# Strassen steps of 512 columns in the down projection, with transfers that add

## The chip, the cores and the metric

The kernel runs on one core of a Trainium2 chip. Its time is the device time of one execution in microseconds. Three runs before the change gave 2172.07, 2172.8 and 2175.01 us, a median of 2172.8 us. The profile is of another single execution.

## The reference: what is computed

The program is a decoder trunk of two layers on 256 tokens of width 2048, all in float32. A layer computes `h = rmsnorm(x)`, projects h by `w_in`, runs latent attention (8 heads) and retention (8 heads) on the parts, joins them, and adds `mixed @ w_o` to x. Then comes the part that the change touches:

```python
h = rmsnorm(x, mlp_norm[l])
x = x + jnp.square(jax.nn.relu(h @ w_up[l])) @ w_down[l]   # 2048 -> 8192 -> 2048
```

After the second layer a last rmsnorm gives the output.

## The kernel before, in words

**Precision by parts.** Weights arrive in float32. Each is split into a rounded head (ScalarE, a cast, L194) and the rest (VectorE, `raw - head`, L195). A product is three partial products: head x head, head x rest, rest x head. In a plain projection (`mac_feat`, L226) head x head and head x rest are one matmul of 512 columns (L228), since the activation tile holds head and rest side by side, 256 tokens each; rest x head is one of 256 columns (L229).

**x and its tiles.** x lies transposed in SBUF: 16 tiles `x[j]` of 128 features by 256 tokens. The inner width of 8192 is handled in four blocks of `FB` = 2048 per layer (loop over b). In each block, 16 up tiles are made in groups of `UP_TILES` = 4: `proj_feat` makes them in PSUM, `relu_sum` joins the two halves and applies relu, `next_u` squares, scales and splits them into `us[k]`. For each two of them `next_f` makes the token-side sums that Strassen's scheme needs (`fs`). The last group is late: its tiles are finished while the down projection starts.

**The down projection of a block.** Part of its 2048 output columns goes by Strassen's seven products, the rest by plain tiles.
- A Strassen step takes two row tiles of `w_down` (256 rows) and 2 x `SB` columns. `second_factors` (L699) loads the two rows of blocks into two `raw` buffers, splits w11, w21 and w22, forms four sums in place on VectorE (L715) and splits those. `seven_products` (L721) runs 7 x 3 matmuls of `SB` columns (L729) into seven PSUM banks. A block has 8 steps.
- After each step stands one plain tile of 128 columns (`next_tile`, L806): two loads of 512 KB, two splits, 16 pairs of matmuls, then a join (L246, L247) and an add into `x[j]` (L811). With `SB` = 384 the steps cover 6 column tiles, and 10 tiles are plain: eight stand between the steps, two after them. In the last block seven stand between, two after `join_products`, one after `add_blocks`.
- After the last step of a block `gather_products` adds the seven banks to seven SBUF sums (copies in the first block). In a layer's last block `join_products` forms the result and `add_blocks` transposes it on TensorE and adds it to x; `done_x` then prepares x for the next stage.

**Buffers and order.** All weights pass through five `raw` buffers (`N_RAW`), filled by SP's queue in program order as buffers come free, and seven buffers of split weights (`N_SPLIT`). `tmp` has six tiles. Instructions are written in program order, and a scheduler that goes by its own cost estimates sets the order on each engine: among those ready by its estimate, the earlier in the program goes first. On the chip each engine then works strictly in that order. POOL does nothing after the first 39 us.

Of the kernel before, what the change touches and what calls it, by code (L numbers as in the profile page):

```python
# [15 lines left out]
ALU = mybir.AluOpType  # L16
# [16 lines left out]

UP_TILES = 4
OUT_GROUPS = [(0, 4), (4, 4), (8, 4), (12, 2), (14, 2)]


SB = 384
SN = 2 * SB // P
TILE_AFTER, LAST_TILE_AFTER = range(8), range(7)  # L40
N_RAW, N_SPLIT = 5, 7

# [51 lines left out]
def kernel(ctx: ExitStack, tc: tile.TileContext, xt, positions, w_in, w_uq, w_ukv, w_o, w_up, w_down,  # L94
# [20 lines left out]
    def w_tile(shape, moving=False):  # L115
        n = math.prod(shape[1:])
        o = MOVING if moving else 0
        t = wpool.tile([P, max(n, 2048) + 2 * MOVING], F32R, tag="w", name="w", bufs=N_SPLIT)[:, o:o + n]
        names = "abc"[:len(shape) - 1]
        return t.rearrange(f"p ({' '.join(names)}) -> p {' '.join(names)}", **dict(zip(names, shape[1:])))  # L120
# [229 lines left out]
    for l in range(DEPTH):  # L350
# [305 lines left out]
        with tc.tile_pool(name=f"mlp{l}", bufs=1) as up:  # L656
# [42 lines left out]
            def second_factors(r0):  # L699


                raws = [w_load(w_down[l][r0 + k * P:r0 + (k + 1) * P, 0:2 * SB], [P, 1, 2 * SB])[:, 0, :] for k in range(2)]
                w11, w12, w21, w22 = (r[:, n * SB:(n + 1) * SB] for r in raws for n in range(2))
                out = []
# [6 lines left out]

                parts([w11], w11)
                parts([w21, w22], raws[1])
                for dst, other in ((w11, w12), (w12, w22), (w22, w11), (w21, w22)):
                    nc.vector.tensor_tensor(dst, dst, other, op=ALU.add)  # L715
                parts([w11, w12], raws[0])
                parts([w21, w22], raws[1])
                weave()
                return out

            def seven_products(ps, us, f, k, factors, first, last):  # L721


                w11, w21, w22, t1, t3, t4, t2 = factors
                a11, a12, a22 = us[2 * k][:, :, 0:P], us[2 * k + 1][:, :, 0:P], us[2 * k + 1][:, :, P:T]
                s1, s3, s2, s4 = (f[:, :, i, :] for i in range(4))
                for i, a, w in ((1, a11, w11), (2, a12, w21), (3, s4, w22), (5, s1, t1), (7, s3, t3), (6, s2, t2), (4, a22, t4)):
                    for n, (p, q) in enumerate(((0, 0), (0, 1), (1, 0))):
                        nc.tensor.matmul(ps[i], a[:, p, :], w[:, q, :], start=first and n == 0, stop=last and n == 2)  # L729

            def gather_products(ps, sums, first):
                for i in (1, 2, 3, 5, 7, 6, 4):
                    if first:
# [27 lines left out]
            for b in range(FF // FB):  # L761
# [21 lines left out]

                for c in range(0, FB - UP_TILES * P, UP_TILES * P):
                    if end and c == UP_TILES * P:
                        add_blocks(join_products(sums, sums), False)
                    for i, ps in enumerate(proj_feat(w_up[l], 0, b * FB + c, ms, UP_TILES)):
                        next_u(relu_sum(ps))
                        if i % 2:
                            next_f()  # L790
                pss = proj_feat(w_up[l], 0, (b + 1) * FB - UP_TILES * P, ms, UP_TILES)
                factors = second_factors(b * FB)
# [13 lines left out]
                def next_tile():  # L806
                    j = tiles.popleft()
                    ps, = proj_feat(w_down[l], b * FB, j * P, us, 1)
                    t = tmp()
                    join(ps, t)  # L810
                    nc.vector.tensor_tensor(x[j], x[j], t, op=ALU.add)  # L811
                    if end:
                        done_x(j)

                pp = {i: bank()[:, 0:SB] for i in (1, 2, 3, 5, 7, 6, 4)}
                steps = FB // (2 * P)
# [68 lines left out]
```

## Time and profile before

| what | value |
|---|---|
| median of three runs | 2172.8 us |
| profiled execution, its own time | 2171.46 us |
| its span, first to last instruction | 2169.7 us |
| TensorE busy | 2140.7 us (99%) |
| VectorE busy | 1770.0 us (82%) |
| ScalarE busy | 1275.3 us (59%) |
| POOL busy | 24.2 us (1%) |
| transfer engines, SP's queue | 61.4% of 16 engines' span |

PE is TensorE, PEld its weight loads, DVE VectorE, ACT ScalarE. Matmuls are pipelined, so a matmul's own duration (0.39 us for 512 columns) is longer than the distance to the next one's start. The distance counts.

### The profile page before, as it was taken

The page shows a single profiled execution, that of the slowest core. Times are in us where ns is not written, and L with a number is a line of the kernel's source. Part 1 is how long each engine was busy: PE and PEld are TensorE (multiplying, and loading weights), DVE is VectorE, ACT ScalarE, POOL GpSimd, SP SyncE. Part 2 cuts the span into 40 slices and gives each one's busy share as a digit, 9 for nine tenths or more (in the row PEclk, how much of TensorE's full clock was granted, in tenths as well). Part 3 has the DMA queues.
Part 4 walks back from the last instruction along what each step waited for, and adds up shares of the span by engine and source line. Part 5 has one row for each costly group of instructions (what it writes and reads, how often), then busy time and mean ns, then how long its engine had stood idle before and what let it go on. Part 6 is the DMA issues. An engine that isn't in the chain of part 4 may idle for free.

```text
span 2169.7 us, 33889 instructions
## 1 busy us (share of the span) xinstructions
PE 2140.7 (99%) x12422; PEld 1915.4 (88%) x12422; DVE 1770.0 (82%) x3335; ACT 1275.3 (59%) x2234; POOL 24.2 (1%) x34
## 2 busy tenths in 40 slices
PE   7999999999999999999999999999999999999998
PEld 6888888889888889988988888888898898898897
DVE  8878976789679779879978888676896896798797
ACT  7555545566565566566655555456665665655665
POOL 4000000000000000000000000000000000000000
PEclk9999999999999999999999999999999999999999
DMA  8555556656756855864675565566486477567554
GB/s 248 179 161 177 146 189 195 184 147 204 233 151 182 241 165 170 250 179 136 206 209 154 169 176 159 185 190 184 136 250 195 143 211 230 147 192 228 168 170 139
DMA packets 367846, 400.16 MB, mean 184 GB/s; under 512 B 13120, under 2 KB 271296, under 8 KB 367680
## 3 DMA queue, kind: packets, MB, share of 16 engines
q1 hardware_dynamic: 366720, 397.08, 61.4%
q8 instruction: 97, 1.59, 0.3%
q10 hardware_dynamic: 960, 0.92, 0.1%
q14 instruction: 69, 0.57, 0.1%
HBM read 395.85 MB, written 2.10 MB: 183 GB/s over the span
## 4 chain that ended last, share of the span: by engine, by line
PE 86%; DVE 8%; ACT 3%; issue 1%; DMA 1%; SPq 0%; ACTq 0%; DVEq 0%
PE mm L228 45%; PE mm L229 24%; PE mm L729 6%; DVE w L195 3%; PE mm L233 3%; DVE raw L715 2%; PE mm L234 1%; PE at L228 1%; ACT w L194 1%; PE at L229 1%; DMA raw<-w_in 1%; ACT tb L246 1%; DVE t L767 1%; PE at L499 0%; PE at L498 0%
## 5 line engine op out<-in xcount | busy, mean ns | idle before, releaser
L194 ACT CAST w<-raw 128x1024 fp32r<-128x1024 f32 (+5 forms) x952 | 871.2, 932 | 694.2 <-PE mm L229 393.4
L195 DVE TENSOR_TENSOR w<-raw,w 128x1024 fp32r<-128x1024 f32 (+4 forms) x952 | 1014.5, 1079 | 305.7 <-ACT w L194 296.9
L228 PE MATMUL mm<-xs,w 128*128 128x512 f32 x2944 | 1033.5, 394 | 9.2 <-ACT w L194 7.5
L229 PE MATMUL mm<-xs,w 128*128 128x256 f32 x2944 | 825.9, 281 | 5.1 <-DVE w L195 4.9
L228 PEld LDWEIGHTS mm<-xs,w 128*128 128x128 f32 x2944 | 553.2, 188 | 129.1 <-ACT w L194 7.8
L229 PEld LDWEIGHTS mm<-xs,w 128*128 128x128 f32 x2944 | 554.8, 189 | 8.1 <-DVE w L195 7.6
L228 PE MATMUL mm<-u,w 128*128 128x512 f32 x1280 | 448.5, 392 | 0.7 <-DVE t L247 0.7
L229 PE MATMUL mm<-u,w 128*128 128x256 f32 x1280 | 360.6, 282 | 4.0 <-DVE w L195 4.0
L228 PEld LDWEIGHTS mm<-u,w 128*128 128x128 f32 x1280 | 240.2, 188 | 50.1 <-DVE t L247 1.0
L229 PEld LDWEIGHTS mm<-u,w 128*128 128x128 f32 x1280 | 241.2, 188 | 8.4 <-DVE w L195 8.0
L228 PE MATMUL mm<-mix,w 128*128 128x512 f32 x512 | 178.0, 392 | 0.0
L246 ACT COPY tb<-mm 128x256 f32<-128x256 f32 x296 | 106.2, 370 | 77.1 <-PE mm L229 72.9
L715 DVE TENSOR_TENSOR raw<-raw 128x384 f32<-128x384 f32 x256 | 142.5, 557 | 6.7
L729 PE MATMUL mm<-w,f 128*128 128x384 f32 x768 | 143.9, 336 | 0.0
L229 PE MATMUL mm<-mix,w 128*128 128x256 f32 x512 | 143.8, 281 | 0.0
L729 PEld LDWEIGHTS mm<-w,f 128*128 128x128 f32 x768 | 134.4, 188 | 0.1
L247 DVE TENSOR_TENSOR t<-mm,tb 128x256 f32<-128x256 f32 x296 | 118.9, 418 | 16.8 <-ACT tb L246 15.3
L729 PE MATMUL mm<-w,u 128*128 128x384 f32 x576 | 121.9, 337 | 0.0
L228 PEld LDWEIGHTS mm<-mix,w 128*128 128x128 f32 x512 | 96.1, 188 | 20.9
L729 PEld LDWEIGHTS mm<-w,u 128*128 128x128 f32 x576 | 98.9, 188 | 2.9 <-ACT w L194 0.3
L229 PEld LDWEIGHTS mm<-mix,w 128*128 128x128 f32 x512 | 96.5, 188 | 0.0
L233 PE MATMUL mm<-w,xs 128*128 128x512 f32 x256 | 92.7, 401 | 0.0
(196 smaller groups left out, 1694.4 us busy)
## 6 DMA issues: line engine op xcount, KB each, us to landing
raw<-w_up SPq DMA_DIRECT2D x256, 512.0 KB, 4.4
raw<-w_down SPq DMA_DIRECT2D x160, 512.0 KB, 5.0
raw<-w_in SPq DMA_DIRECT2D x144, 512.0 KB, 4.5
raw<-w_down SPq DMA_DIRECT2D x128, 384.0 KB, 3.3
raw<-w_o SPq DMA_DIRECT2D x64, 512.0 KB, 4.1
raw<-w_uq SPq DMA_DIRECT2D x16, 384.0 KB, 4.1
raw<-w_in SPq DMA_DIRECT2D x16, 320.0 KB, 3.6
raw<-w_ukv SPq DMA_DIRECT2D x8, 512.0 KB, 4.4
```

The lines of the kernel that those rows point to most:

```text
L194: nc.scalar.copy(dst_h, src)
L195: nc.vector.tensor_tensor(dst_l, src, dst_h.bitcast(F32), op=ALU.subtract)
L228: nc.tensor.matmul(ps, wk[:, 0, n0:n0 + P], act.rearrange("p s t -> p (s t)"), start=first, stop=False)
L229: nc.tensor.matmul(ps[:, 0:T], wk[:, 1, n0:n0 + P], act[:, 0, :], start=False, stop=last)
L233: nc.tensor.matmul(ps, act[:, 0, t0:t0 + P], wk, start=first, stop=False)
L234: nc.tensor.matmul(ps[:, 0:256], act[:, 1, t0:t0 + P], wk[:, 0], start=False, stop=last)
L246: nc.scalar.copy(tb, ps[:, T:2 * T])
L247: nc.vector.tensor_tensor(dst, ps[:, 0:T], tb, op=ALU.add)
L715: nc.vector.tensor_tensor(dst, dst, other, op=ALU.add)
L729: nc.tensor.matmul(ps[i], a[:, p, :], w[:, q, :], start=first and n == 0, stop=last and n == 2)
L767: nc.vector.tensor_tensor(t, t, rows["rs2b"], op=ALU.mult)
```

## The change

- Strassen steps become `SB` = 512 columns wide. They cover 8 column tiles, and 8 are plain: one after each step, none left at the end of a block. In a layer's last block six stand between the steps, one after `join_products`, one after `add_blocks`.
- The sums of the weights are arranged in another way. One of them, w12 + w22, is made by a transfer from HBM that adds into the buffer that holds w12. POOL issues it. Three sums stay on VectorE, now of 512 columns. Casts and subtracts are three of 1024 columns and one of 512 (before: three of 768 and one of 384), and the order of the seven products is new.
- `N_SPLIT` is 6 instead of 7, and one small buffer (`wh`) takes the split of 512 columns.
- The up groups are 4, 4, 4, 2, 2 tiles, so the late group has two.
- A plain tile outside a layer's last block isn't joined on VectorE. ScalarE copies both halves of its bank to SBUF, and two transfers issued by POOL add them to `x[j]`, one after the other.

```diff
@@ -31,14 +31,14 @@
 G_FINAL = DEPTH * G_LAYER
 C_IDENT, C_MASK, C_TRI, C_FREQ, C_PAR, C_KDEC, C_GEPS, C_W = 0, 128, 512, 640, 641, 643, 659, 675
 
-UP_TILES = 4
+UP_GROUPS = [(0, 4), (4, 4), (8, 4), (12, 2), (14, 2)]
 OUT_GROUPS = [(0, 4), (4, 4), (8, 4), (12, 2), (14, 2)]
 
 
-SB = 384
+SB = 512
 SN = 2 * SB // P
-TILE_AFTER, LAST_TILE_AFTER = range(8), range(7)
-N_RAW, N_SPLIT = 5, 7
+TILE_AFTER, LAST_TILE_AFTER = range(8), range(6)
+N_RAW, N_SPLIT = 5, 6
 
 
 
@@ -115,7 +115,8 @@
     def w_tile(shape, moving=False):
         n = math.prod(shape[1:])
         o = MOVING if moving else 0
-        t = wpool.tile([P, max(n, 2048) + 2 * MOVING], F32R, tag="w", name="w", bufs=N_SPLIT)[:, o:o + n]
+        tag, size, bufs = ("wh", 1024, 1) if moving and n <= 1024 else ("w", max(n, 2048), N_SPLIT)
+        t = wpool.tile([P, size + 2 * MOVING], F32R, tag=tag, name=tag, bufs=bufs)[:, o:o + n]
         names = "abc"[:len(shape) - 1]
         return t.rearrange(f"p ({' '.join(names)}) -> p {' '.join(names)}", **dict(zip(names, shape[1:])))
 
@@ -700,7 +701,8 @@
 
 
                 raws = [w_load(w_down[l][r0 + k * P:r0 + (k + 1) * P, 0:2 * SB], [P, 1, 2 * SB])[:, 0, :] for k in range(2)]
-                w11, w12, w21, w22 = (r[:, n * SB:(n + 1) * SB] for r in raws for n in range(2))
+                w11, t3, w21, w22 = (r[:, n * SB:(n + 1) * SB] for r in raws for n in range(2))
+                nc.gpsimd.dma_start(t3, w_down[l][r0 + P:r0 + 2 * P, SB:2 * SB], accum_op=ALU.add)
                 out = []
 
                 def parts(srcs, src):
@@ -709,27 +711,27 @@
                     split_w(ws[:, 0, :], ws[:, 1, :], src)
                     out.extend(ws[:, :, i * SB:(i + 1) * SB] for i in range(len(srcs)))
 
-                parts([w11], w11)
                 parts([w21, w22], raws[1])
-                for dst, other in ((w11, w12), (w12, w22), (w22, w11), (w21, w22)):
-                    nc.vector.tensor_tensor(dst, dst, other, op=ALU.add)
-                parts([w11, w12], raws[0])
-                parts([w21, w22], raws[1])
+                parts([w11, t3], raws[0])
+                for dst, a, b, op in ((w11, w11, t3, ALU.add), (t3, w11, w21, ALU.add), (w22, w11, w22, ALU.subtract)):
+                    nc.vector.tensor_tensor(dst, a, b, op=op)
+                parts([w11, t3], raws[0])
+                parts([w22], w22)
                 weave()
                 return out
 
             def seven_products(ps, us, f, k, factors, first, last):
 
 
-                w11, w21, w22, t1, t3, t4, t2 = factors
+                w21, w22, w11, t3, t2, t4, t1 = factors
                 a11, a12, a22 = us[2 * k][:, :, 0:P], us[2 * k + 1][:, :, 0:P], us[2 * k + 1][:, :, P:T]
                 s1, s3, s2, s4 = (f[:, :, i, :] for i in range(4))
-                for i, a, w in ((1, a11, w11), (2, a12, w21), (3, s4, w22), (5, s1, t1), (7, s3, t3), (6, s2, t2), (4, a22, t4)):
+                for i, a, w in ((2, a12, w21), (3, s4, w22), (1, a11, w11), (7, s3, t3), (6, s2, t2), (4, a22, t4), (5, s1, t1)):
                     for n, (p, q) in enumerate(((0, 0), (0, 1), (1, 0))):
                         nc.tensor.matmul(ps[i], a[:, p, :], w[:, q, :], start=first and n == 0, stop=last and n == 2)
 
             def gather_products(ps, sums, first):
-                for i in (1, 2, 3, 5, 7, 6, 4):
+                for i in (2, 3, 1, 7, 6, 4, 5):
                     if first:
                         sums[i] = up.tile([P, SB], F32, tag=f"p{i}", name=f"p{i}")
                         nc.scalar.copy(sums[i], ps[i])
@@ -781,14 +783,15 @@
                     nc.scalar.activation(t, t, AF.Relu)
                     return t
 
-                for c in range(0, FB - UP_TILES * P, UP_TILES * P):
-                    if end and c == UP_TILES * P:
+                for c, nt in UP_GROUPS[:-1]:
+                    if end and c == 4:
                         add_blocks(join_products(sums, sums), False)
-                    for i, ps in enumerate(proj_feat(w_up[l], 0, b * FB + c, ms, UP_TILES)):
+                    for i, ps in enumerate(proj_feat(w_up[l], 0, b * FB + c * P, ms, nt)):
                         next_u(relu_sum(ps))
                         if i % 2:
                             next_f()
-                pss = proj_feat(w_up[l], 0, (b + 1) * FB - UP_TILES * P, ms, UP_TILES)
+                c, nt = UP_GROUPS[-1]
+                pss = proj_feat(w_up[l], 0, b * FB + c * P, ms, nt)
                 factors = second_factors(b * FB)
                 late = [relu_sum(ps) for ps in pss]
 
@@ -806,13 +809,18 @@
                 def next_tile():
                     j = tiles.popleft()
                     ps, = proj_feat(w_down[l], b * FB, j * P, us, 1)
-                    t = tmp()
-                    join(ps, t)
-                    nc.vector.tensor_tensor(x[j], x[j], t, op=ALU.add)
                     if end:
+                        t = tmp()
+                        join(ps, t)
+                        nc.vector.tensor_tensor(x[j], x[j], t, op=ALU.add)
                         done_x(j)
-
-                pp = {i: bank()[:, 0:SB] for i in (1, 2, 3, 5, 7, 6, 4)}
+                        return
+                    for h in range(2):
+                        t = tmp()
+                        nc.scalar.copy(t, ps[:, h * T:(h + 1) * T])
+                        nc.gpsimd.dma_start(x[j], t, accum_op=ALU.add)
+
+                pp = {i: bank()[:, 0:SB] for i in (2, 3, 1, 7, 6, 4, 5)}
                 steps = FB // (2 * P)
                 for k in range(steps):
                     if k:
```

## Rows read from the trace of the kernel before

**Rows 1.** The page: busy time of TensorE (share, instructions) and the chain by engine.
```profile
PE 2140.7 (99%) x12422; PEld 1915.4 (88%) x12422; DVE 1770.0 (82%) x3335; ACT 1275.3 (59%) x2234; POOL 24.2 (1%) x34
...
PE 86%; DVE 8%; ACT 3%; issue 1%; DMA 1%; SPq 0%; ACTq 0%; DVEq 0%
```

**Rows 2.** TensorE's waits, 467 to 1070 us: total, times, longest.
```profile
PE mm L229 <- DVE w L195: 2.5, 5, 0.8
PE mm L228 <- DVE t L247: 0.7, 1, 0.7
```

**Rows 3.** One stretch: PE, PEld, DVE, ACT, POOL busy us; clock; transfer share; GB/s.
```profile
470.00:540.00 70.00, 69.62 (x401) 64.46 (x400) 66.46 (x110) 44.37 (x75) 0.00 (x0) 1.00 0.62 183
```

**Rows 4.** The chain in order of time: start, length, what.
```profile
1571.48 3.65 PE mm L729 x21
```

**Rows 5.** TensorE's timeline, last block: start, length, instructions.
```profile
2136.76 0.40 PE L228 MATMUL mm<-u,w 128*128 128x512 f32 x1
2136.99 0.28 PE L229 MATMUL mm<-u,w 128*128 128x256 f32 x1
...
2142.32 0.40 PE L228 MATMUL mm<-u,w 128*128 128x512 f32 x1
...
2147.88 1.47 PE L755 MATMUL at<-cst,p 128*128 128x128 f32 x12
2149.10 0.48 PE L228 MATMUL mm<-u,w 128*128 128x512 f32 x1
```

**Rows 6.** Groups by line and shape: count, busy us, mean ns, idle before.
```profile
L195 DVE TENSOR_TENSOR w<-raw,w 128x1024 fp32r<-128x1024 f32 x632 | 767.6, 1226 | 292.1 <-ACT w L194 289.1 <-PE mm L228 0.5 <-issue 0.3
L194 ACT CAST w<-raw 128x1024 fp32r<-128x1024 f32 x632 | 658.4, 1049 | 459.8 <-PE mm L229 364.6 <-PE mm L234 26.5 <-issue 19.8
...
L195 DVE TENSOR_TENSOR w<-raw,w 128x768 fp32r<-128x768 f32 x192 | 183.1, 954 | 8.7 <-ACT w L194 2.9
...
L715 DVE TENSOR_TENSOR raw<-raw 128x384 f32<-128x384 f32 x256 | 142.5, 557 | 6.7
...
L247 DVE TENSOR_TENSOR t<-mm,tb 128x256 f32<-128x256 f32 x296 | 118.9, 418 | 16.8 <-ACT tb L246 15.3
L246 ACT COPY tb<-mm 128x256 f32<-128x256 f32 x296 | 106.2, 370 | 77.1 <-PE mm L229 72.9 <-DVE t L247 3.7
...
L195 DVE TENSOR_TENSOR w<-raw,w 128x384 fp32r<-128x384 f32 x64 | 35.3, 552 | 0.0
...
L195 DVE TENSOR_TENSOR w<-raw,w 128x512 fp32r<-128x512 f32 x16 | 11.0, 690 | 0.9 <-ACT w L194 0.9
...
L194 ACT CAST w<-raw 128x512 fp32r<-128x512 f32 x16 | 9.9, 618 | 7.5 <-PE mm L229 7.5
```

**Rows 7.** Transfer issues, whole run: KB each, median us to landing.
```profile
raw<-w_down SPq DMA_DIRECT2D x160, 512.0 KB, 5.0
...
out<-x SPq DMA_DIRECT2D x1, 128.0 KB, 1.8
```

**Rows 8.** The same view for single loads, issued at 692.8 and 718.4 us.
```profile
raw<-w_down SPq DMA_DIRECT2D x1, 384.0 KB, 3.0
...
raw<-w_up SPq DMA_DIRECT2D x1, 512.0 KB, 3.7
```

**Rows 9.** ScalarE's timeline, 680 to 704 us; in brackets idle time before, and releaser.
```profile
687.85 0.83 ACT L194 CAST w<-raw 128x768 fp32r<-128x768 f32 x1 [2.17 <-DMA raw<-w_down]
690.85 0.84 ACT L194 CAST w<-raw 128x768 fp32r<-128x768 f32 x1 [2.16 <-DVE raw L715]
...
695.91 0.83 ACT L194 CAST w<-raw 128x768 fp32r<-128x768 f32 x1 [0.47 <-DMA raw<-w_down]
699.39 0.84 ACT L194 CAST w<-raw 128x768 fp32r<-128x768 f32 x1 [2.64 <-DVE raw L715]
```

**Rows 10.** Timeline of all engines, 24 to 27 us.
```profile
24.37 1.76 DVE L195 TENSOR_TENSOR w<-raw,w 128x1024 fp32r<-128x1024 f32 x1
...
25.14 1.26 POOL L166 TENSOR_SCALAR tab<-tab 128x256 f32<-128x256 f32 x1
```

## The prediction

> **What bounds the kernel now.** I read the page's busy line and chain first [rows 1]. TensorE is busy 2140.7 of 2169.7 us, and 86% of the chain that ended last is its matmuls, so what counts is the time from one matmul's start to the next one's, not a matmul's own modelled duration. I then asked for TensorE's waits in the first layer's four down projections [rows 2]: 3.2 us in 600. Nothing holds TensorE back there, but the stretch view of one such block shows how little room there is [rows 3]: VectorE is busy 66.46 of 70 us, the granted clock is 1.00 (the 2.4 GHz level, so no clock is to be won), and the transfer engines are busy 0.62. So every matmul column removed shows in the time, as long as VectorE and the weight loads still stay ahead.
>
> **TensorE's columns.** One Strassen step is 21 matmuls of 384 columns, 3.65 us on the chain [rows 4], 0.174 us apiece. At 512 columns I take the spacing after an L228 matmul of that width, 2136.99 - 2136.76 = 0.23 us [rows 5]: 21 x 0.23 = 4.83 us, 1.18 more. A block has 8 steps and the kernel 8 blocks: 64 x 1.18 = +75.5 us. The wider steps replace two of ten plain tiles in each block. A tile is 16 k-pairs and takes 2142.32 - 2136.76 = 5.56 us [rows 5]: 16 tiles are -89.0 us. Two more column tiles pass through the transposes at each layer's end, 8 transposes more in all at (2149.10 - 2147.88)/12 = 0.10 us: +0.8 us. Net -12.7 us. Were the 512-column spacing 0.005 us dearer (the rows give it to two places), 1344 matmuls would take back 6.7 us; cheaper by as much, they'd add it.
>
> **VectorE in a step with its tile.** Now [rows 6]: subtracts 3 x 0.954 + 0.552, four sums 4 x 0.557, the tile's two subtracts 2 x 1.226, its join 0.418 and its add to x of the same shape, in all 8.93 us in a step of 3.65 + 5.56 = 9.21. After: 3 x 1.226 + 0.690, three sums of 512 columns (0.557 + 0.137 for 128 more columns, about 0.69 each) 2.07, and the tile's 2.45; join and add leave, outside each layer's last block: 8.89 us in a step of 10.39. VectorE goes from 97% to 86%. ScalarE comes to 5 x 1.049 + 0.618 + two copies of 0.370 = 6.6 us and is far from full. The short waits of rows 2 come from VectorE being late; both layers have about twice 3.2 us. I take 3 us back (0 to 6).
>
> **The last up group of two.** Only two up tiles stay late instead of four. Their three VectorE passes of 256 columns each (0.42) and one factor set of six passes leave the crowded first step: 2.5 to 5 us of VectorE per block, say 4, which becomes lead over TensorE at step 1. TensorE's columns there are the same.
>
> **The accumulate for w12 + w22.** No row shows such a transfer. It starts when the first weight buffer has landed and must end before that buffer's cast. From below it is the 1.8 us of the smallest plain transfer to landing (128 KB), from above the 5.0 us median of the 512 KB loads [rows 7]; I take 3.6 us, near the single loads of 384 and 512 KB that head a burst [rows 8]. What hides it: the first buffer of a step is asked for well before the second, because with five buffers the second is asked for only when the step before frees one. ScalarE now stands 2.2 and 0.5 us waiting for that second load [rows 9]. The accumulate thus runs beside a wait that is there anyway. Cover gone, its excess falls on the loop below.
>
> **The loop of weight buffers.** From one cast of the sums to the next, 690.85 to 699.39, are 8.54 us [rows 9]: cast, subtract, load 3.0 [rows 8], cast, subtract, three sums. At 512 columns: 1.05 + 1.23 + load 3.7 (the 512 KB row [rows 8]) + 1.05 + 1.23 + two sums 1.39 + 0.3 of hand-overs = 9.95 us, if the accumulated buffer is split while the other loads, as w11 is now. If it's split after, one subtract more: 11.2. A step takes 10.39. At the far end the loop loses 0.8 us a step over six steps, 4.8 us a block, which the 4 us of lead nearly cover. I take nothing (0 to +7 for eight blocks).
>
> **The accumulates to x.** 96 transfers of 128 KB replace 48 joins and adds of VectorE. Nothing on TensorE waits for them: x is read again only in the layer's last block. Their cost is their place in POOL's queue (rival below) and traffic: 256 + 256 KB beside 2048 KB per step, or twice that if the old value is read too. In 10.39 us that's 252 to 303 GB/s; at 183 GB/s for a 0.62 share [rows 3] a share of 0.85 to 1.0. I take 0.85 and no cost, with loads of 5.0 us (the loaded median of rows 7) instead of 3.7 as the bad end.
>
> **What ends a block.** No plain tile is left after the seven gathers. They are 7 x 0.69 = 4.8 us beside the last step's tile, 5.56 us, and VectorE's spare 1.5. At each layer's end eight x tiles instead of six come out of the join, each with three VectorE passes of 0.42 or more, and one plain tile fewer covers them: 2 x 1.3 us more, partly hidden. I take +1.5 us per layer, +3 in all (0 to +6).
>
> **Sum.** -12.7 - 3 + 3 = -12.7 us. The profiled execution took 2171.46 us (span 2169.7 and 1.8 around it), 1.3 below the median of 2172.8, so the forecast is 2158.8 against its own time and 2160 beside the median; I give 2159. Its own bounds: 2171.5 - 12.7 - 6.7 - 6 = 2146 and 2171.5 - 12.7 + 6.7 + 7 + 6 = 2179, not all at once: 2150 to 2169.
>
> One rule speaks against the accumulates. In the first 35 us POOL computes, and there a 1024-column subtract of VectorE takes 1.76 us instead of 1.226 [rows 6, 10]. The Trainium skill, SBUF — State Buffer, Who interferes with whom, says that a VectorE instruction with two SBUF inputs contends with a GpSimd instruction that reads SBUF, and infers that writing descriptors for a transfer doesn't. The rows agree with the first half; none shows the second. By the inference the sum stands. Without it, rival 3.
>
> **Rivals.**
> 1. The buffer loop becomes the bound. With transfers dense, loads take 5.0 us and the accumulated buffer is split last: 12.5 us per turn against 10.39, over six steps 12.7 us, less 4 of lead, 8.7 per block, +70: 2229. With slow loads alone the loop is 11.25, 5.2 us over six steps, 1.2 a block, +10: 2169; loads halfway slow and the late split give 11.85, 4.8 a block, +38: 2197. For it: ScalarE already waits for this load [rows 9]. Against: VectorE has 1.5 us of slack per step that it lacks now. Chance 0.16, most of it at 2169 to 2197.
> 2. The other side: POOL's queue. A plain tile's two accumulates write the same x, so the second can't be issued until the first has landed, and a next step's w12 + w22 may be queued behind both. With a per transfer: tile end + 0.74 of copies + 2a until that sum has landed, then cast, subtract, two sums, cast, subtract, 5.9 us, against 10.39 + 2.8 until TensorE wants the product of these sums. It decides from a = 3.3 us; beyond, each step loses 2(a - 3.3). At 3.6 that's 0.6 x 48 = 29 us, 2188; at 5.0, 163 us, 2322. For it: in the program the tile's transfers stand ahead of the next step's. Against: that sum belongs to the step after next, its weights are loaded early, and so it should be ready and issued first. Chance 0.14.
>    The Trainium skill, DMA: Bandwidth & Descriptors, Anatomy of one DMA, gives a GpSimd-issued transfer 2.0 us plus its bytes at 436 GB/s, by estimate 2.3 us for 128 KB; this rival would then cost nothing. No run here shows it.
> 3. POOL's issues slow VectorE. Three per step; if each blocks as in rows 10, 3 x 0.5 us: VectorE 10.4 us in a step of 10.39. The slack and the 3 us of waits are gone, a few tenths per step lost: 2162 to 2176, say 2169. Chance 0.08.
>
> **How the numbers follow.** The forecast gets 0.62. This measurement can tell about 0.2%, 4.3 us: faster is below 2168.5, slower above 2177. Faster: 0.60 of the forecast, 0.02 of rival 1, 0.03 of rival 3, 0.65. Same: 0.02 + 0.04 + 0.04 = 0.10. Slower: 0.10 of rival 1, 0.14 of rival 2, 0.01 of rival 3, 0.25. The range 2150 to 2196 leaves out the far ends of rivals 1 and 2.
>
> **What would show it.** Step products of 4.83 us in the chain and 10.39 us from step to step; VectorE near 0.87 of a down block; TensorE's waits no more than now. The accumulated buffer's cast waiting for a transfer from POOL, with TensorE waiting behind it, would be rival 2; step distances of 11 us and more with the wait at the second load, rival 1; subtracts of 1.5 us, rival 3. A spacing off 0.23 us for 512 columns would make the first term wrong by itself.

## The result, and the profile after

The changed kernel takes 2260.1 us, median of four runs (2252.6 to 2263.2), against 2173.0 us for the kernel before beside it: ratio 1.0396, 95% interval 1.0383 to 1.0409. The forecast was 2159 with a range to 2196: wrong, on the other side of zero.

In the page of after (the profile of the changed kernel), TensorE's share and the chain by engine answer to [rows 1]:

```profile
PE 2172.7 (96%) x11926; PEld 1866.1 (83%) x11926; DVE 1749.5 (77%) x3119; ACT 1294.6 (57%) x2234; POOL 163.7 (7%) x194
...
PE 64%; DVE 14%; DMA 11%; ACT 6%; issue 3%; ACTq 0%; SPq 0%; DVEq 0%; POOLq 0%
PE mm L229 33%; PE mm L230 17%; DMA raw<-w_down 11%; DVE w L196 7%; ACT w L195 5%; DVE raw L717 3%; PE mm L234 3%; PE mm L731 3%; PE mm L235 1%; PE at L229 1%; DMA raw<-w_in 1%; PE at L230 1%; DVE u L189 1%; DVE t L769 0%; PE at L500 0%
```

TensorE's part of the chain fell from 86 to 64%; loads of `w_down`, which the chain before hardly had, hold 11%, and the splits stand beside them (lines of after: casts L195 on ScalarE, subtracts L196 and sums L717 on VectorE, Strassen products L731, the sum's transfer L705, the transfers to x L821). TensorE's waits in after, with total, times and longest:

```profile
PE mm L731 <- DVE w L196: 30.9, 47, 0.8
PE mm L731 <- ACT w L195: 22.9, 30, 1.2
PE mm L230 <- DVE w L196: 12.5, 6, 5.2
```

The Strassen products, L731, have 53.8 us of short waits. In the kernel before they have none; its few waits in [rows 2] stand at plain tiles. The stretch of [rows 3] again, and two stretches of the next block, in the same columns:

```profile
470.00:540.00 70.00, 67.27 (x336) 55.52 (x335) 52.64 (x65) 36.76 (x54) 12.91 (x15) 1.00 0.81 211
650.00:682.00 32.00, 32.00 (x165) 27.06 (x164) 23.08 (x33) 17.26 (x28) 4.37 (x5) 1.00 0.75 203
682.00:746.00 64.00, 54.98 (x244) 42.60 (x243) 44.37 (x49) 30.17 (x42) 12.18 (x14) 0.95 0.77 191
```

VectorE got the room that was forecast (52.64 of 70 us, before 66.46), and TensorE stands idle more all the same. A block begins well, 32.00 of 32, and fails from its fourth step on. TensorE's timeline shows it, with the first Strassen product of each of six steps:

```profile
661.53 0.86 PE L731 MATMUL mm<-w,u 128*128 128x512 f32 x3
...
671.97 0.86 PE L731 MATMUL mm<-w,u 128*128 128x512 f32 x3
...
682.41 0.39 PE L731 MATMUL mm<-w,u 128*128 128x512 f32 x1
...
695.95 1.08 PE L731 MATMUL mm<-w,u 128*128 128x512 f32 x3
...
708.81 0.39 PE L731 MATMUL mm<-w,u 128*128 128x512 f32 x1
...
723.90 0.86 PE L731 MATMUL mm<-w,u 128*128 128x512 f32 x3
```

Two distances of 10.44, then 13.54, 12.86 and 15.09 us. ScalarE's timeline of the same steps, to be held against [rows 9]:

```profile
693.93 2.00 ACT L195 CAST w<-raw 128x1024 fp32r<-128x1024 f32 x2 [3.86 <-DMA raw<-w_down]
698.94 1.04 ACT L195 CAST w<-raw 128x1024 fp32r<-128x1024 f32 x1 [3.01 <-DVE raw L717]
699.89 0.61 ACT L195 CAST wh<-raw 128x512 fp32r<-128x512 f32 x1
...
707.45 2.00 ACT L195 CAST w<-raw 128x1024 fp32r<-128x1024 f32 x2 [4.51 <-DMA raw<-w_down]
712.46 1.04 ACT L195 CAST w<-raw 128x1024 fp32r<-128x1024 f32 x1 [3.01 <-DVE raw L717]
```

The reader is to see a loop; one turn of it here is 707.45 - 693.93 = 13.52 us. The second load lands, both buffers are cast and split, three sums follow, and ScalarE casts the first buffer's sums at 698.94. VectorE subtracts behind that cast:

```profile
700.02 1.23 DVE L196 TENSOR_TENSOR w<-raw,w 128x1024 fp32r<-128x1024 f32 x1 [0.58 <-ACT w L195]
```

Only with its end, 701.25, is a buffer free for the next step's second load. From landing to free buffer that makes 7.3 us. The load itself, issued there, and the transfers of the page:

```profile
raw<-w_down SPq DMA_DIRECT2D x1, 512.0 KB, 6.1
```

```profile
raw<-w_down SPq DMA_DIRECT2D x256, 512.0 KB, 6.2
...
raw<-w_down POOLq DMA_DIRECT2D x64, 256.0 KB, 4.1
x<-t POOLq DMA_DIRECT2D x96, 128.0 KB, 5.1
```

7.3 + 6.1 and a hand-over are the 13.5 us, more than the 10.45 that TensorE needs. The steps at a block's start run on what lay ready. The step at 708.81 has three waits of 0.6 to 0.9 us:

```profile
709.82 0.73 PE L731 MATMUL mm<-w,u 128*128 128x512 f32 x2 [0.61 <-DVE w L196]
...
713.56 0.49 PE L731 MATMUL mm<-w,f 128*128 128x512 f32 x1 [0.90 <-ACT w L195]
714.82 1.18 PE L731 MATMUL mm<-w,f 128*128 128x512 f32 x2 [0.77 <-DVE w L196]
```

Around the last of them the granted clock falls to the lower level (1.2 GHz) for a while, which makes the loss larger than the waits. The same shows in a later block, behind waits of 0.90 and 0.76 us (clock in the column before the transfer share):

```profile
716.50:720.00 3.50, 3.50 (x15) 2.83 (x15) 1.22 (x2) 0.00 (x0) 0.01 (x1) 0.74 0.81 214
889.00:893.00 4.00, 4.00 (x12) 3.17 (x13) 2.74 (x3) 1.48 (x3) 0.88 (x1) 0.58 0.90 188
```

Over the profiled run the mean clock is 0.989 (before 0.998): by estimate 0.009 of 2261 us, up to 20 us.

### The profile page after: what moved, and what is told of

Read it like the earlier page. It is cut to its first block, busy times and chain, and to the rows that moved or that the text cites. A ratio compares the mean times of both kernels' runs of the same rounds, so it can differ in the third digit from the quotient of the medians.

```text
span 2261.4 us, 33076 instructions
## 1 busy us (share of the span) xinstructions
PE 2172.7 (96%) x11926; PEld 1866.1 (83%) x11926; DVE 1749.5 (77%) x3119; ACT 1294.6 (57%) x2234; POOL 163.7 (7%) x194
## 4 chain that ended last, share of the span: by engine, by line
PE 64%; DVE 14%; DMA 11%; ACT 6%; issue 3%; ACTq 0%; SPq 0%; DVEq 0%; POOLq 0%
PE mm L229 33%; PE mm L230 17%; DMA raw<-w_down 11%; DVE w L196 7%; ACT w L195 5%; DVE raw L717 3%; PE mm L234 3%; PE mm L731 3%; PE mm L235 1%; PE at L229 1%; DMA raw<-w_in 1%; PE at L230 1%; DVE u L189 1%; DVE t L769 0%; PE at L500 0%
## 5 line engine op out<-in xcount | busy, mean ns | idle before, releaser
L196 DVE TENSOR_TENSOR w<-raw,w 128x1024 fp32r<-128x1024 f32 (+2 forms) x856 | 992.1, 1173 | 427.8 <-ACT w L195 421.5
L195 ACT CAST w<-raw 128x1024 fp32r<-128x1024 f32 (+2 forms) x856 | 851.3, 1007 | 754.7 <-PE mm L230 336.6
L229 PE MATMUL mm<-u,w 128*128 128x512 f32 x1024 | 363.7, 395 | 0.0
L230 PE MATMUL mm<-u,w 128*128 128x256 f32 x1024 | 290.6, 284 | 6.1 <-DVE w L196 5.9
L229 PEld LDWEIGHTS mm<-u,w 128*128 128x128 f32 x1024 | 195.3, 191 | 43.0
L731 PE MATMUL mm<-w,f 128*128 128x512 f32 x576 | 175.3, 410 | 49.3 <-DVE w L196 26.1
L230 PEld LDWEIGHTS mm<-u,w 128*128 128x128 f32 x1024 | 195.5, 191 | 13.1 <-DVE w L196 10.2
L731 PEld LDWEIGHTS mm<-w,f 128*128 128x128 f32 x576 | 105.2, 188 | 97.7 <-DVE w L196 39.8
L731 PE MATMUL mm<-w,u 128*128 128x512 f32 x576 | 174.4, 407 | 5.1 <-DVE w L196 4.8
L705 POOL DMA_DIRECT2D raw<-w_down x64 | 56.0, 875 | 1635.5 <-DMA raw<-w_down 654.5
L731 PEld LDWEIGHTS mm<-w,u 128*128 128x128 f32 x576 | 105.5, 192 | 33.9 <-DVE w L196 11.1
L717 DVE TENSOR_TENSOR raw<-raw 128x512 f32<-128x512 f32 x192 | 127.6, 689 | 3.5
L229 PEld LDWEIGHTS mm<-mix,w 128*128 128x128 f32 x512 | 96.1, 188 | 20.8
L821 POOL DMA_DIRECT2D x<-t x96 | 83.7, 872 | 402.9 <-ACT w L195 133.2
```

Source lines behind the costliest of these rows:

```text
L195: nc.scalar.copy(dst_h, src)
L196: nc.vector.tensor_tensor(dst_l, src, dst_h.bitcast(F32), op=ALU.subtract)
L229: nc.tensor.matmul(ps, wk[:, 0, n0:n0 + P], act.rearrange("p s t -> p (s t)"), start=first, stop=False)
L230: nc.tensor.matmul(ps[:, 0:T], wk[:, 1, n0:n0 + P], act[:, 0, :], start=False, stop=last)
L705: nc.gpsimd.dma_start(t3, w_down[l][r0 + P:r0 + 2 * P, SB:2 * SB], accum_op=ALU.add)
L717: nc.vector.tensor_tensor(dst, a, b, op=op)
```

## The experiments

All times are medians beside runs of the kernel before (2172.3 to 2173.0 us in each group). In the table, t 5 and t 6 are the buffers for t; edits are shown shortened. e6, e12 and e16 leave out or misplace a part of a sum, so they serve for time alone.

| kernel | order of splits and sums | w12 + w22 | x | weight buffers | us | ratio, 95% interval |
|---|---|---|---|---|---|---|
| after | new | adding transfer | transfers | 5 | 2260.1 | 1.0383 to 1.0409 |
| e1 | old | VectorE | VectorE | 5 | 2173.8 | 0.9992 to 1.0011 |
| e2 | new | adding transfer | VectorE | 5 | 2255.6 | 1.0352 to 1.0400 |
| e3 | old | VectorE | transfers | 5 | 2172.1 | 0.9988 to 1.0007 |
| e4 | new | adding transfer | transfers | 6, t 5 | 2226.6 | 1.0227 to 1.0269 |
| e5 | first buffer first | adding transfer | transfers | 5 | 2229.1 | 1.0250 to 1.0278 |
| e6 | new | plain transfer | transfers | 5 | 2224.6 | 1.0227 to 1.0257 |
| e9 | new | VectorE | transfers | 5 | 2204.4 | 1.0127 to 1.0158 |
| e10 | new | adding transfer | VectorE | 6, t 5 | 2171.8 | 0.9992 to 1.0010 |
| e11 | new | VectorE | transfers | 6, t 5 | 2197.9 | 1.0104 to 1.0131 |
| e12 | new | half of it | transfers | 5 | 2228.3 | 1.0243 to 1.0271 |
| e13 | new | adding transfer | transfers | 6, t 6 | 2212.6 | 1.0172 to 1.0210 |
| e14 | new | VectorE | transfers | 6, t 6 | 2179.5 | 1.0022 to 1.0046 |
| e15 | new | adding transfer | one per tile | 6, t 6 | 2177.0 | 1.0014 to 1.0033 |
| e16 | new | adding transfer | two, other tiles | 6, t 6 | 2184.6 | 1.0034 to 1.0068 |

### Which part costs: e1, e2, e3, e4

e1 is the change without its transfers and its order of sums; e2 is after with x on VectorE; e3 is after with the old sums; e4 has one buffer more.

```diff
 e1, e3: second_factors, seven_products and the products' order as before, at SB = 512
 e1, e2: a plain tile:  join(ps, t); nc.vector.tensor_tensor(x[j], x[j], t, op=ALU.add)
 e4:    -N_RAW, N_SPLIT = 5, 6       +N_RAW, N_SPLIT = 6, 6
        -tmp(tag="t", bufs=6), tmp("sq", 2)   +tmp(tag="t", bufs=5), tmp("sq", 1)
```

> The 512-column steps, the new up groups and buffers are kept; the sums of the weights are all made by VectorE in the old arrangement (w11 split first), and plain tiles are joined and added by VectorE. No transfer adds anything. Theory A (the loop of five weight buffers, lengthened by slow loads): without added transfers the second load takes about 3.7 us again, the loop is 3.7 + 6.9 = 10.6 us against a step of 10.45, and VectorE is nearly full: 2165 to 2185 us. Theory B (the added transfers themselves are what TensorE waits for): 2155 to 2170. Theory C (512 columns themselves, whatever feeds them): about 2260.

> The changed kernel with plain tiles joined and added by VectorE, so only w12 + w22 is made by a transfer. Theory A: the sum's transfer still meets the second load, the load takes 5 us or more, the loop 12.5 to 13 us: 2215 to 2245. Rival: the transfers to x are to blame (POOL's queue and their traffic): 2160 to 2175.

> The changed kernel with all four weight sums on VectorE in the old arrangement, so only the plain tiles' adds go by transfers. Theory A: the first buffer is split while the second loads, so the loop is a load of 4 to 4.5 us + 6.9 = about 11.2 us: 2175 to 2205. Rival (the transfers to x are to blame): about 2250.

> The changed kernel with six weight buffers instead of five (room taken from one tile of t and one of sq). All transfers stay. Theory A: the second load no longer waits for the buffer of the step before, the loop is cut: 2160 to 2185, TensorE's waits in the down projections below 15 us. Theory B (transfers that land late, POOL's queue): no change, 2250 to 2265.

The wider step alone and the transfers to x, with the old sums, cost and win nothing, with steps of 10.45 us throughout. The sum by transfer with its new order costs all of it: e2 lies even above the range of its Theory A, e3 below. e4 falls between its two ranges: one buffer more gives 33 us back, not all. In e1 the columns' gain goes at the layer's end: TensorE's timeline there, the stretch of the wait and the stretch behind it show one wait of 6.43 us and then half clock:

```profile
1083.48 0.58 PE L230 MATMUL mm<-u,w 128*128 128x256 f32 x1 [6.43 <-DVE w L196]
```

```profile
1076.00:1083.00 7.00, 1.05 (x6) 0.53 (x4) 7.00 (x19) 5.74 (x16) 0.00 (x0) 0.81 0.00 0
1083.00:1087.00 4.00, 3.52 (x11) 3.03 (x12) 4.00 (x7) 0.52 (x2) 0.00 (x0) 0.50 0.47 130
```

### Order or transfer: e9, e6, e12, e5

```diff
 e9  -nc.gpsimd.dma_start(t3, w_down[l][r0 + P:r0 + 2 * P, SB:2 * SB], accum_op=ALU.add)
      parts([w21, w22], raws[1])
     +nc.vector.tensor_tensor(t3, t3, w22, op=ALU.add)
 e6  -... SB:2 * SB], accum_op=ALU.add)   +... SB:2 * SB])
 e12 -dma_start(t3, ... SB:2 * SB]        +dma_start(t3[:, 0:SB // 2], ... SB:SB + SB // 2]
 e5  +parts([w11, t3], raws[0]); w11 += t3; parts([w21, w22], raws[1])
     +w21 = w11 + w21; w22 = w11 - w22; parts([w11], w11); parts([w21, w22], raws[1])
```

> The changed kernel with one thing undone: the sum w12 + w22 is made by VectorE again, in place, before the first pair is split; the new order of splits and sums (second buffer first, all three other sums after both splits) and the transfers that add to x stay. Theory A, the order: from the landing of the second load to the issue of the next the buffers now wait for cast 1.05, subtract 1.1, sum 0.6, cast 1.05, subtract 1.1, three sums 2.0, cast and subtract 1.6, some 8.5 us, and with a load of 5.0 us that is a turn of 13.5 us, more than the 10.45 us that TensorE needs for a step: 2235 to 2270 us, steps of 12.5 to 13.5 us from the fourth on. Theory B, the adding transfer itself (its late landing, and its packets beside the second load): without it the steps are 10.45 us and the time is that of the kernel with 512 columns alone, 2168 to 2180 us. Between 2190 and 2230: both have a share.

> The changed kernel with the sum's transfer made a plain one: it writes w22 over w12 and adds nothing (the addition is left out, so the products with that sum are others). Bytes written, queue, issue and waits are the same; only what the packets do is less. Theory B1, the adding packets (each takes about twice a plain one: 178 against 84 ns for 2048 bytes) hold up the second load, which goes back from 6.2 to about 5.0 us, and land earlier: 2200 to 2235 us. Theory A, the order of splits and sums with five buffers sets the turn, and a load of 6.2 or 5.2 us is a small part of it: 2245 to 2262 us, with steps still 12 to 14 us.

> The changed kernel with the sum's transfer adding only the first 256 of its 512 columns (128 KB in place of 256 KB; the other half of that sum is left out, so its products are others). Waits, queue, order and number of transfers stay. Theory B1, the bytes: what the transfer costs beyond the order (2260.1 against 2204.4 us) is the time that its packets take from the second load, so half the bytes give about half: 2225 to 2240 us, and the loads of w_down land in about 5.8 us in place of 6.2. Rival B2, the transfer as such (its issue behind the first load's landing, its place in the queue, its fixed landing time): 2245 to 2260 us.

> The changed kernel, both kinds of adding transfers kept, with another order: the first pair (w11 and the transferred sum) is split first, w11 + sum follows, then the second pair is split; the last two sums are written into the second buffer, so the first is free after one more split and not after all of them. Theory A, the order: the buffer that the next second load waits for comes free some 3 us earlier, the turn falls from 13.5 to about 10.5 us, the steps go back to 10.45 to 11 us and the time to 2165 to 2200 us. Theory B, the transfer: the sum's transfer still lands 4 us or more after the first load and ScalarE now waits for it first with everything queued behind it, so nothing is won: 2240 to 2290 us.

e9 fell between its theories: the order has a share of its own, 2204.4 - 2172.1 (e3) = 32 us. ScalarE's timeline of e9 has the same loop with a shorter load:

```profile
695.34 2.00 ACT L195 CAST w<-raw 128x1024 fp32r<-128x1024 f32 x2 [2.61 <-DMA raw<-w_down]
700.35 1.05 ACT L195 CAST w<-raw 128x1024 fp32r<-128x1024 f32 x1 [3.01 <-DVE raw L717]
...
706.80 2.00 ACT L195 CAST w<-raw 128x1024 fp32r<-128x1024 f32 x2 [2.44 <-DMA raw<-w_down]
```

706.80 - 695.34 = 11.46 us, of which 7.3 again from landing to free buffer, so the load is about 4.2 with its hand-over. The expectation had put 8.5 us where 7.3 were measured, having lined up what runs beside each other on two engines. The plain transfer brings 20 us more, the addition another 36; half the bytes leave 2228.3, as the theory of bytes had it (2225 to 2240). The second load that follows the freed buffer, at the same place of a step near 700 to 711 us, shows the same order: 4.0 us in e9, 4.7 with the plain transfer (e6), 4.9 with half the addition (e12), 6.1 in after. What differs is in the transfer queues from 680 to 716 us, with packets, MB and their packets' time as a share of 16 engines, first of e10, whose POOL queue (q0) carries nothing but these sums:

```profile
q1 hardware_dynamic: 7607, 7.17, 62.4%
q0 software_dynamic: 432, 0.79, 13.6%
```

A MB by an adding transfer takes packet time of 13.6/0.79 = 17.2 points (per cent) of that share, a MB of loads 62.4/7.17 = 8.7: half as much. After's window, with x added too, says the same, 17.6 against 9.5:

```profile
q1 hardware_dynamic: 6247, 5.41, 51.3%
q0 software_dynamic: 1248, 1.51, 26.6%
```

Packet time isn't the same as an engine's occupation: in after the share reaches 1.16 from 720 to 724 us. That the addition costs the load beside it is shown by e6 against after.

e5 frees a buffer earlier and won 31 us of the 87, not the 60 and more that its Theory A expected. Now the first cast waits for the adding transfer, which lands 5.5 us (the page's median) after an issue that must itself wait for the first load: issued at 694.62 us and landed 6.0 us later, with the cast at 700.66.

### The sixth buffer, and what then comes last: e10, e11, e13 to e16

```diff
 e10: e4 with x on VectorE;  e11: e9 with e4's buffers;  e15, e16: on e13
 e13: after with N_RAW = 6, tmp("sq", 1), tmp("tb", 2) and t at 6;  e14: e9 with the same
 e15  -for h in range(2): t = tmp(); nc.scalar.copy(t, ps[:, h * T:(h + 1) * T]); dma_start(x[j], t, ...)
      +t = tmp(); join(ps, t); nc.gpsimd.dma_start(x[j], t, accum_op=ALU.add)
 e16  -dma_start(x[j], t, ...)            +dma_start(x[SN + (j - SN + 4 * h) % 8], t, ...)
```

> The changed kernel with two things altered: six buffers for loaded weights in place of five (paid with one buffer less for t and one less for squares), and the plain tiles joined and added to x by VectorE again; the sum by an adding transfer and the new order stay. With six buffers and x by transfers the kernel took 2226.6 us, and there the sum's transfer stood behind two transfers for x in POOL's queue and landed up to 8 us late. Theory C, the queue: what six buffers did not give back is the sum's transfer behind those of x, so without them 2170 to 2190 us, nearly all steps 10.45 us. Rival A, the loop of buffers alone (load and 7.4 us of splits and sums): it is broken by the sixth buffer in either kernel, x on VectorE changes nothing or adds its share of VectorE, and the time stays at 2215 to 2240 us, with the sum's transfer still landing too late because it can only be issued when the first load has landed.

> The kernel with the new order whose sum VectorE makes in place (2204.4 us), with six buffers for loaded weights in place of five (and one buffer less for t and for squares). There the steps from the sixth on take 11.1 to 11.7 us, which is the second load, 4.2 us, and 7.2 us from its landing to the subtract that frees the buffer for the next such load. Theory A: that loop is what its 31 us are; a sixth buffer lets the load be issued a part of a step earlier, the steps are 10.45 us and the time is that of 512 columns alone: 2168 to 2178 us. Rival D: not the buffers but the engines' order (ScalarE stands 3.0 us in each step for the sums, VectorE's queue behind them), which a sixth buffer does not change: 2195 to 2206 us.

> The changed kernel, with both kinds of adding transfers and its order, and six buffers for loaded weights; this time the sixth is paid with one buffer less for squares and one less for tb, and t keeps its six. With t at five the same kernel took 2226.6 us, and there VectorE waited six times, up to 4.6 us, for a t buffer that a transfer to x still read. Theory E, the t buffers: that wait is all that stood between that kernel and the one with x on VectorE (2171.8 us), so with six of them 2170 to 2185 us. Theory C, POOL's queue: the sum's transfer stands behind those for x whatever t has, so 2210 to 2230 us.

> The new order with its sum on VectorE, x by transfers, six buffers for loaded weights, paid with one buffer less for squares and one less for tb; t keeps its six. With t at five it took 2197.9 us. Theory E, the t buffers: the loop of five weight buffers was all of this order's 31 us, and t's five were what remained: 2168 to 2178 us. Rival D, the order on ScalarE and VectorE itself: 2190 to 2204 us.

> The changed kernel with six buffers for loaded weights and six for t (2212.6 us), with the two halves of a plain tile joined by VectorE and added to x by one transfer in place of two. Theory F, the pair in series: the two transfers of a tile add to the same x tile, so the second waits on POOL until the first has landed, some 6 us, and the sum's transfer of a later step stands behind it; with one transfer nothing waits: 2170 to 2182 us. Rival G, the load of the transfer engines by everything together: half of the x bytes gone gives back about half of the 41 us that stand between that kernel and the one with x on VectorE: 2188 to 2200 us.

> The same kernel (2212.6 us) with two transfers for each plain tile as before, but the second half goes to another tile of x, four tiles on (so those sums are others than the reference's). Number, bytes and order of the transfers stay; only the second no longer adds to what the first is still adding to, and waits for no landing. Theory F, the pair in series: 2170 to 2185 us. Rival G, the load of the transfer engines: unchanged, 2205 to 2218 us.

e10 gives all 84 us of e2 back with one buffer more, new order and all, and its steps are 10.47 and 10.49 us where after has 13.54 and 12.86:

```profile
685.42 0.86 PE L731 MATMUL mm<-w,u 128*128 128x512 f32 x3
...
695.91 0.86 PE L731 MATMUL mm<-w,u 128*128 128x512 f32 x3
...
706.38 0.86 PE L731 MATMUL mm<-w,u 128*128 128x512 f32 x3
```

So the loop of buffers was the bound, and the sum by transfer then costs nothing. With x by transfers the sixth buffer isn't enough, for two reasons; e11 fell into the range of its rival D (the order itself), but for the first of these reasons, as e14 shows. One was mine: in e4 I had paid with a t buffer, and VectorE's waits show that it was missed, since a t is held until its transfer lands:

```profile
DVE t L694 <- DMA x<-t: 21.4, 6, 4.6
```

With six t the times fall by 14 us (e13 against e4) and 18 us (e14 against e11). e14 is 1.5 us above its Theory E, and e13 in the range of its Theory C: the t buffers weren't all. The other reason is POOL's queue. Its timeline in e13:

```profile
845.05 0.87 POOL L821 DMA_DIRECT2D x<-t  x1 [3.80 <-ACT t L820]
852.21 0.89 POOL L821 DMA_DIRECT2D x<-t  x1 [6.30 <-ACT w L195]
852.92 1.09 POOL L705 DMA_DIRECT2D raw<-w_down  x1
```

The transfer issued at 845.05 took 6.5 us to land:

```profile
x<-t POOLq DMA_DIRECT2D x1, 128.0 KB, 6.5
```

The second transfer of the tile goes out at 852.21, 0.7 us behind that landing (the releaser named in the bracket had long been done), and the sum's transfer stands behind it. Both add to the same tile of x; the Trainium skill, DMA: Bandwidth & Descriptors, Rules for kernel authors, says that an adding transfer beside another access of the same bytes must wait for the earlier one's semaphore, and the trace shows such a wait. In e16 the second half goes to another tile, and the two leave together:

```profile
840.68 1.75 POOL L821 DMA_DIRECT2D x<-t  x2 [1.55 <-ACT t L820]
848.88 0.89 POOL L705 DMA_DIRECT2D raw<-w_down  x1 [6.45 <-DVE raw L717]
```

Same bytes, same order, 28 us less: of the 41 us between e13 and e10 the pair in series is about two thirds. e15, with one transfer per tile and so half the bytes as well, reaches 2177.0. What the rest is, 7 us in e14 over e3 and 13 us in e16 over e10, stays open; the bytes beside the loads would fit, and no run isolates them.

### Looking for a faster version: b1 to b4

```diff
 b1 (on e1), b3 (on e10):
 -LAST_TILE_AFTER = range(6)                     +range(5)
 -while len(tiles) > 1: next_tile()              +while len(tiles) > 2: next_tile()
 -add_blocks(blocks)                             +add_blocks(blocks, halves=[0]); next_tile(); add_blocks(blocks, halves=[1])
 b2: e3 with that, and the last block's first five tiles added by transfers, done_x one step later
 b4: b3 with LAST_TILE_AFTER = (0, 2, 4, 6)
```

> No transfer that adds: 512 columns alone (2173.7 us), with the end of a layer put otherwise: one plain tile fewer after the steps, and the eight blocks added to x in two halves with a plain tile between them. In the kernel with 512 columns alone TensorE stands still 6.4 us at a layer's end, for a weight split that VectorE has behind eight additions, eight norm products and eight sums of squares (some 10 us of it in one piece), and another 2.8 us behind the last tile. Theory: in halves each piece is 5.3 us beside a tile of 5.6 us, so 6 to 9 us come back: 2164 to 2168 us. Rival: VectorE is the bound of the whole stretch, the wait moves to the next layer's first tiles: 2171 to 2175 us.

> 512 columns, the four sums on VectorE in the old order, the plain tiles added to x by transfers (2172.1 us), with the end of a layer altered: there the first five tiles too are added to x by transfers, and their norm product and square follow one step later; the eight blocks are added in two halves with a tile between. In the last block of the first layer VectorE is busy 97 to 99% of 1000 to 1060 us with 512 columns alone, so it sets that stretch: halves alone only moved its wait (2174.0 us). Theory: each of the five tiles takes 0.67 us of joins off VectorE, 3.3 us in all, and the wait of 6.4 us is cut: 2165 to 2170 us. Rival: the transfers' landing holds up ScalarE's queue where the norm products wait for them, or the stretch is bound elsewhere: 2171 to 2178 us.

> The kernel with the sum by an adding transfer, x on VectorE and six buffers for loaded weights (2171.8 us), with the end of a layer in halves: one plain tile fewer after the steps, the eight blocks added to x in two halves with a tile between. With 512 columns alone VectorE was busy 97 to 99% of the first layer's last block and halves only moved the wait; here the sum's transfer leaves it 16.4 of 20 us just ahead of the layer's end. Theory: the wait of 4.5 us at the layer's end goes, and with it the stretch at half clock after it: 2164 to 2168 us. Rival: it moves, as before: 2170 to 2174 us.

> As the one before it, with the four tiles that stand among the last block's steps put after steps 0, 2, 4 and 6 and four left behind the steps, two of them ahead of the blocks' additions. Theory: VectorE's 13 us of joins and additions stand beside 22 us of tiles and all of TensorE's waits at the layer's end go: 2162 to 2167 us. Rival: the steps without a tile need some 5.9 us of VectorE in 4.9 us, so what the end gains the steps lose: 2170 to 2176 us.

b1 took 2174.0 us (0.9998 to 1.0016), nothing. b2 took 2219.1 (1.0210 to 1.0238), far above its rival's range, but by the mechanism that the rival named: ScalarE's queue stands behind norm products and squares of x tiles that haven't landed:

```profile
ACT xs L191 <- DMA x<-t: 31.7, 5, 7.0
ACT sq L272 <- DMA x<-t: 21.0, 4, 6.2
```

b3 took 2170.0 us, ratio 0.9986 (0.9977 to 0.9995): the interval excludes 1, but the gain is less than the 0.2% that the prediction set as the least to be told, and less than expected; 2170.0 is the lower edge of its rival's range. The stretch that stood at half clock in e1 stays at the upper level in b3:

```profile
1083.00:1087.00 4.00, 3.51 (x19) 2.85 (x19) 3.94 (x9) 2.06 (x6) 0.00 (x0) 1.00 0.44 133
```

b4 took 2178.7 us (1.0019 to 1.0044), above its rival's 2176 too. The rival's mechanism shows: in the first layer's last block two steps with one tile between take 15.5, 18.4 and 19.4 us, where 10.45 + 4.89 would be 15.3.

## Why the prediction was wrong

**The step that failed** is "The loop of weight buffers", taken as nothing: 9.95 us per turn against 10.39. The turn was 13.5. Rival 1 named this mechanism (12.5 us, 2229 us at its far end) with a chance of 0.16, most of it at 2169 to 2197, and was itself too low. Two terms were mis-sized. The load was put at 3.7 us, the price of a load that heads a burst [rows 8]; here it is 6.1. And the buffer that receives the sum was taken to be split while the second load runs, as w11 is now; the new order splits it after (in the diff `parts([w21, w22], raws[1])` stands first), which the text had priced at 11.2 us and then dismissed. With the two, 2.4 and 1.2 us, the 9.95 become 13.6. e9 shows the late order by itself (turn 11.46, +32 us against e3), e6 and e12 the load, e10 that a sixth buffer ends it.

**The accumulate for w12 + w22** was put at 3.6 us to landing and hidden beside the wait for the second load. It lands in 4.1 us, well inside the bounds, and in the steps shown no cast waits for it (the two casts at 693.93 stand without a gap). What was missing is that it runs while that second load runs and lengthens it: 6.1 us, against 4.7 beside a plain transfer (e6) and 4.0 beside none (e9). A cost was looked for where it is waited for, and stood in the loop beside it. The sum of traffic (a share of 0.85 to 1.0, of which 0.85 was taken) didn't show it either: the share is 0.75 to 0.81 over the stretches shown, but the loads come in bursts after each freed buffer, and it goes from 0.43 (712 to 716.5 us) to 1.16 (720 to 724).

**Rival 2, POOL's queue**, decided from 3.3 us per transfer to x, and 5.1 were measured, but with five buffers x by transfers costs only 2260.1 - 2255.6 = 4.5 us beside the sum, with overlapping intervals. That what it delays is waited for anyway is argued, not shown. The mechanism is real and appears once the loop is broken (e13 against e16). **Rival 3** is refuted: VectorE's 1024-column subtract takes 1.225 us in after, 1.226 before [rows 6], with 160 issues on POOL:

```profile
L196 DVE TENSOR_TENSOR w<-raw,w 128x1024 fp32r<-128x1024 f32 x792 | 960.4, 1225 | 421.4 <-ACT w L195 415.2 <-PE mm L230 4.8
```

**The accumulates to x** cost nothing by themselves, as forecast (e3).

**TensorE's columns**: the 21 Strassen products that start at 661.53 us are followed by the next tile at 666.42, so they take 4.89 us, 0.233 each. At 0.23 + 0.0033 the 1344 matmuls are 4.5 us dearer, inside the bound named there: about -8 us in place of -12.7.

**What ends a block** was put at +1.5 us per layer. At the first layer's end it is one wait of 6.43 us, a shorter one and the half clock between them. TensorE's timelines of before and e1 give the balance, from the first Strassen product of one block to that of the next. The six stretches between blocks of one layer are 11.3 us shorter in e1, 1.9 each, near the 2.0 that the forecast's -12.7 - 3 would be over eight blocks: what the columns lack, the waits give, since one or two steps in each block of before take 9.6 to 10.3 us among steps of 9.2, some 8 us in all in place of 3, and in e1 all take 10.45. From the first layer's last block to the second layer's first it is 557.1 us in place of 546.5, and the way to the end is 2.3 us longer. The two layer ends so take all of it back, and e1 comes out at no change (interval -1.7 to +2.4 us). In e1 VectorE is busy 19.77 of 20 us from 1000 us on, in that layer's last block, and eight additions with their norms come on top. So the forecast would have been some 13 us low even with the loop right (e10: 2171.8), and that part was sized wrong at the layers' ends.

## What to carry to other kernels

Write out the loop through which a buffer comes back (free, issue, landing, each split and sum until the last reader) with the loaded price of a transfer, and compare it with the step before counting any engine's busy share: here VectorE had 14 points of room by the forecast, and with x on VectorE one buffer too few cost 84 us (e2 against e10). A transfer moved to another queue is not hidden because nobody waits for it; here it lengthened the load beside it, and what it holds (a t buffer, a place in POOL's queue) until it lands counts as well. In e13 two transfers that add to one tile follow one another by a whole landing time, 6.5 us.

## What the runs showed of the hardware

- The packets of a transfer that adds take about twice as long per byte as those of a plain load (17.2 against 8.7 points of share per MB in e10), and the load beside it took 6.1 us in place of 4.7 beside a plain transfer (after, e6).
- The Trainium skill, DMA: Bandwidth & Descriptors, Anatomy of one DMA, gives a transfer issued by GpSimd 2.0 us plus its bytes at 436 GB/s, by estimate 2.6 us for 256 KB. The page of e6 has 3.1 us for the plain one, that of after 4.1 for the adding one, both beside loads.
- POOL's issues, 0.87 us each, left VectorE's 1024-column subtracts at 1.225 us (1.226 before).
- In these traces the granted clock fell to the lower level after one long wait (6.43 us; 0.50 from 1083 to 1087 us of e1) and also around a few waits of less than 1 us close together (0.74 in the 3.5 us from 716.5, 0.58 from 889 to 893 us of after).
